# Sharing weight tiles between two streams in the input projection of a hybrid diffusion layer

## The chip, the cores and the metric

The kernel runs on one core of a Trainium2 chip. A core has five engines with instruction queues of their own, each of which is worked off in order: TensorE (PE, matmuls into the accumulator memory PSUM, with its weight loads PEld beside it), VectorE (DVE), ScalarE (ACT, activation functions with loadable tables), GpSimd (POOL, which doesn't reach PSUM) and SyncE (SP), which here issues nearly all DMAs. PSUM has eight banks of 128 x 512 float32. The metric is the time of one execution on the device in microseconds, the median of the runs.

## The reference

One layer runs on two groups of tokens with the same weights: a prompt of 256 tokens and a sample of 1024. Each has a modulation vector, a projection into 24 tiles of 128 channels and 16 dt channels, a gated short convolution, a bidirectional state space scan and an output projection, then a gated feed-forward part with a convolution. Cut to what matters here:

```python
mod_ctx = (jax.nn.silu(c_ctx)[None] @ w_ada[i] + b_ada[i])   # prompt
mod_lat = (jax.nn.silu(c) @ w_ada[i] + b_ada[i])             # sample; six blocks of 1024 each
h = rmsnorm(x, g_norm1) * (1.0 + scale_m) + shift_m
proj = h @ w_in
hc, gb, gc, z, xbc, dtf, dtb = jnp.split(proj, offs, axis=-1)
out_a = gb * dwconv1d(gc * hc, w_conv_short)
xbc = jax.nn.silu(dwconv1d(xbc, w_conv_ssd, b_conv_ssd))
xs, bm, cm = jnp.split(xbc, [SSD_WIDTH, SSD_WIDTH + SSD_GROUPS * D_STATE], axis=-1)
dt_f = jax.nn.softplus(dtf + dt_bias[0]); dt_b = jax.nn.softplus(dtb + dt_bias[1])
y_f, s_f = ssd_scan(xh, dt_f, a[0], bm, cm, init_f)
y_b_rev, s_b = ssd_scan(xh[:, ::-1], dt_b[:, ::-1], a[1], bm[:, ::-1], cm[:, ::-1], init_b)
y = rmsnorm((y_f + y_b_rev[:, ::-1] + xh * d_skip) * jax.nn.silu(z), g_ssd_norm)
x = x + gate_m * (jnp.concatenate([out_a, y], axis=-1) @ w_out)
h2 = rmsnorm(x, g_norm2) * (1.0 + scale_f) + shift_f
u = conv(h2 @ w_up); ug, uv = jnp.split(u, 2, axis=-1)
x = x + gate_f * ((jax.nn.silu(ug) * uv) @ w_down)
```

The kernel returns the normalised outputs of both streams and the prompt's two final states.

## The kernel before

Channels lie on the 128 partitions, tokens along the free dimension. Every float32 operand of a projection is split into a high part that the matmul takes in full and a low remainder, and `mm3` adds three products (high x high, high x low, low x high) over eight slices of 128 input channels. A weight tile (512 KB) is brought in by `wload`: a DMA into a "raw" tile (two buffers), a copy on ACT to the high part and a subtraction on DVE or POOL for the low part. The parts rotate over three pairs of buffers, whi and wlo twice and whx and wlx once. A prompt tile is 24 matmuls of 256 tokens, a sample tile 48 of 512.

The program is traced in the order in which it is written; a planner of the kernel language then sets the order of each engine's instructions from its own estimate of when each is ready, with the written order as priority. `after(a, b)` asks for a behind b without a wait on the chip. A tile that reuses a buffer waits until its last user is done; a pool opened on the bytes of closed pools waits for all their users, or, with `reuse_waits="tile"`, tile by tile (in PSUM: bank by bank).

The stages in question, in the order written:

- The loop over eight channel slices normalises, modulates with blocks 0 and 1 (`ada_block`), and already accumulates the sample's X tiles 0 and 1 and its dt projection. The normalised prompt lies in "bc" tiles (its high and low parts), the sample in "h".
- `xbc(SS, i)` evacuates the sample's X tiles 0 and 1: a convolution of three taps, one ACT pass and two DVE passes. PSUM then holds "acc" (two buffers of two banks), "sa" (three of one bank) and "yp" (one).
- The prompt (`SP`) runs through all its 24 tiles in a row, each with its own `wload`, staged in one of eight "x" tiles of the pool `nrm`: X, B and C (8), z (4, `zproj`), the short convolution (`outa`, 3 tiles each for j = 0 to 3). Its accumulators are "sa" for the first two and "acc" for the rest. `dtstage` computes softplus and the cumulative sums of dt (a chain of some 20 small DVE and ACT instructions on 40 partitions), `dttok` transposes them to token order on TensorE and forms the decays. For the prompt dtstage is written behind the first z tile, dttok behind `outa` 0. The sample's dtstage is written at the end.
- The sample (`SS`) runs through tiles 2 to 6 of X, B and C, with modulation blocks 2 to 5 between them (`ada`: 8 DMAs of 512 KB a block into the "x" tiles, matmuls in four column groups, and for each half of a block an ACT copy, four transposes and a reduction). dttok of the sample comes behind tile 4.
- `nrm` closes, the scan begins: `ssd_pass1(SP)`, the sample's tile 7, `ssd_pass1(SS)` and `ssd_pass2`, filled up with the sample's z and short convolution tiles (`fillers`).
- The pool ps1 closes; ps2 opens for the output projection (`wout`) and the feed-forward part.

Of the kernel before, what the change touches and what calls it, by code (L numbers as in the profile page):

```python
# [33 lines left out]
N_LOOP = 2  # L34
# [21 lines left out]
def body(nc, tc, A):  # L56
    cnt = [0]

    def T(pool, shape, tag, bufs, dt=F32):
        cnt[0] += 1  # L60
        return pool.tile(list(shape), dt, tag=tag, bufs=bufs, name=f"{tag}_{cnt[0]}")

    def open_pool(name, side="left", **kw):
        if "space" not in kw:
            kw["reuse_waits"] = "tile"
        g = tc.tile_pool(name=name, bufs=1, side=side, **kw)
        return g, g.__enter__()
# [27 lines left out]
    def smv(n):  # L95
        a, b = SMO[n]
        return sm[:, a:b]
# [26 lines left out]
    wx = [nrm]  # L124
    g_ps, ps = open_pool("ps1", space=PSUM)

    def pacc():
        return T(ps, [P, 1024], "acc", 2)

    def pst():  # L130
        return T(ps, [P, 512], "yp", 1)
# [1 line left out]
    def psa():  # L133
        return T(ps, [P, 512], "sa", 3)
# [11 lines left out]
    def wload(src, lo_eng, raw=None):  # L146
        if raw is None:
            raw = T(wst, [P, KT, P], "raw", 2)
        dma(raw, src)
        hi, lo = wpair()  # L150
        act(hi, raw, AF.Copy)  # L151
        tt(lo, raw, hi.bitcast(F32), ALU.subtract, lo_eng)
        return hi, lo
# [12 lines left out]
        return mms  # L166


    def ada(cc, wt):
        pt = [psa(), psa()]  # L170
        for k0 in (0, 4):
            ws = [wt() for _ in range(4)]
            for q, w in enumerate(ws):
                dma(w, A["w_ada"][(k0 + q) * P:(k0 + q + 1) * P, (cc - 2) * 1024:(cc - 1) * 1024])
            for i in range(2):
                for q in (3, 2, 1, 0):
                    nc.tensor.matmul(pt[i][32 * q:32 * q + 32, :], sc[:, k0 + q, :],
                                     ws[q][:, i * 512:(i + 1) * 512], start=k0 == 0, stop=k0 == 4,
                                     skip_group_check=True, tile_position=(0, 32 * q))
        ss = []  # L180
        for i in range(2):
            s = T(nrm, [P, 1024], "x", 8)
            act(s[:, 0:512], pt[i], AF.Copy)
            ss.append(s)
        yield
        for i, s in enumerate(ss):
            tp = psa()
            for b in range(4):
                mm = nc.tensor.transpose(tp[:, b * P:(b + 1) * P], s[:, b * P:(b + 1) * P], ident)
                if i == b == 0:  # L190
                    after(mm, mid_mm[0])
            b0 = cc * 8 + i * 4
# [48 lines left out]
    pr_p = pst()  # L241
    for i in range(2):
        nc.tensor.matmul(pr_p[:, 0:TP], ones, accp[:, i], start=i == 0, stop=i == 1)
    xs = [T(nrm, [P, TS], "x", 8) for _ in range(KT)]
    pr_s = [psa(), psa()]
    for k in range(KT):
        dma(xs[k], xT[:, k, TP:TT])
# [108 lines left out]

    last_mm, mid_mm = [], [None]

    def proj(s, m, lo_eng):
        g = proj_halves(s, m, lo_eng)  # L360
        next(g)
        return next(g)

    def proj_halves(s, m, lo_eng):
        s.n += 1
        wh, wl = wload(A["w_in"][m], lo_eng, T(nrm, [P, KT, P], "x", 8) if s.name == "p" else None)
        pp = psa() if s.name == "p" and s.n <= 2 else pacc()
        outs = []
        for a, b in s.chunks:
            outs.append((pp[:, a:b], (lambda k, a=a, b=b: s.hi(k)[:, a:b]),  # L370
                         (lambda k, a=a, b=b: s.lo(k)[:, a:b])))
        ks = list(range(KT))
        for half in (ks[0:KT // 2], ks[KT // 2:]):
            ends = mm3(outs, wh, wl, KT, half)
            mid_mm[0] = ends[0]
            last_mm.append(ends[-1])
            yield pp[:, 0:s.T]

    def conv1d_sb(out, u, w, n):
        stt(out[:, 1:n], u[:, 0:n - 1], w[0], out[:, 1:n], ALU.mult, ALU.add)  # L380
        stt(out[:, 0:n - 1], u[:, 1:n], w[2], out[:, 0:n - 1], ALU.mult, ALU.add)

    def xbc(s, i, out, lo_eng):
        w = [smv("wcx")[:, i * 3 + t:i * 3 + t + 1] for t in range(3)]
        b = smv("bcx")[:, i:i + 1]
        if s.name == "s" and i < N_LOOP:
            u = pps[i]
            for c in range(2):
                act(out[:, c * 512:(c + 1) * 512], u[c], AF.Identity, scale=w[1], bias=b)
            stt(out[:, 1:513], u[0], w[0], out[:, 1:513], ALU.mult, ALU.add)  # L390
            stt(out[:, 513:TS], u[1][:, 0:511], w[0], out[:, 513:TS], ALU.mult, ALU.add)
            stt(out[:, 0:511], u[0][:, 1:512], w[2], out[:, 0:511], ALU.mult, ALU.add)
            stt(out[:, 511:TS - 1], u[1], w[2], out[:, 511:TS - 1], ALU.mult, ALU.add)
        else:
            pp = proj(s, 16 + i, lo_eng)
            act(out, pp, AF.Identity, scale=w[1], bias=b)
            conv1d_sb(out, pp, w, s.T)

    def zproj(s, j, lo_eng):
        for _ in zproj_halves(s, j, lo_eng):  # L400
            pass
# [186 lines left out]
    def ssd_pass2(s, fill, post):  # L588
# [110 lines left out]
    d4_s = dtcopy(SS, pd_s)  # L699
    for i in range(N_LOOP):  # L700
        xbc(SS, i, SS.X[i], PG)
        act(SS.X[i], SS.X[i], AF.Silu)
    for i in range(8):
        xbc(SP, i, (SP.X + bcp)[i], PG if i % 3 else PV)
        if i == 5:
            pd_p = [psa()]
            dtmm(pd_p, range(KT), lambda k: xp[k // 4][:, k % 4], TP)
            d4_p = dtcopy(SP, pd_p)
    act(xall, xall, AF.Silu)
    silu = act(bcall, bcall, AF.Silu)  # L710
    for j in range(4):
        zproj(SP, j, PG if j % 2 else PV)
        if j == 0:
            dts = dtstage(SP, d4_p, silu)
    for j in range(4):
        for _ in outa(SP, j, PG):
            pass
        if j == 0:
            dttok(SP, *dts)
    dts = dtstage(SS, d4_s, silu)  # L720


    bcs = [T(sd, [P, TS], "bc", 4) for _ in range(4)]
    SS.B, SS.C = bcs[0:2], bcs[2:4]
    xbcs = SS.X + bcs

    def silu_s(i):
        after(act(xbcs[i], xbcs[i], AF.Silu), SS.last_exp)

    pend = None  # L730
    for i in range(N_LOOP, 7):
        xbc(SS, i, xbcs[i], PV)
        if pend is not None:
            next(pend)
            pend = None
        if i == 4:
            dttok(SS, *dts)
            for k in range(N_LOOP, 4):
                silu_s(k)
        if i >= 4:  # L740
            silu_s(i)
        if i < 6:
            pend = ada(i, lambda: T(nrm, [P, 1024], "x", 8))
            next(pend)
    make_aff(1, 4, "g2")
    wx[0] = None
    close_pool(g_nrm)
# [498 lines left out]
```

## Time and profile before

| | us |
|---|---|
| median of 3 runs | 1577.9 (1575.82 to 1578.37) |
| profiled execution | 1575.34 |
| its span, first to last instruction | 1573.4 |
| PE busy | 1522.2 |
| DVE busy | 1104.6 |
| ACT busy | 662.1 |
| POOL busy | 514.6 |

The profiled execution is one of the same program; its span is what the views of the trace count from. "Busy" is the time in which an engine has an instruction under way; matmuls overlap, so a matmul's own duration is longer than its share, and the distance from one start to the next tells what it costs. A row of a group or a timeline reads: line, engine, operation, out<-in by the names of tiles, shape, count, and in square brackets the idle time before it and what ended that. The granted clock is TensorE's, 1.00 at full speed.

### The profile page before, as it was taken

Reading aid. Unit: us, or ns where it says so; the run is one execution under the profiler, and the core shown is the slowest. Engines: PE = TensorE matmul, PEld = TensorE weight load, DVE = VectorE, ACT = ScalarE, POOL = GpSimd, SP = SyncE. Lnnn points to the kernel's source line nnn. Section 1 sums busy time; section 2 is a strip of 40 time slices with the busy share of each in tenths; the row PEclk is TensorE's granted clock in tenths of the full one; section 3 lists DMA queues with packets and bytes.
Section 4 is the critical chain, followed back from the end, with each engine's and each line's share of the span. In section 5 each row is a group of like instructions: output and inputs, shape, how many; then the busy total and the mean of one; then the engine's idle time right before and its main releaser. Section 6 shows DMA issues by size and latency. Waiting matters only on the chain. (4 is left out here: it accounts for less than half of the span.)

```text
span 1573.4 us, 22518 instructions
## 1 busy us (share of the span) xinstructions
PE 1522.2 (97%) x8722; PEld 1296.7 (82%) x8722; DVE 1104.6 (70%) x1634; ACT 662.1 (42%) x1025; POOL 514.6 (33%) x288
## 2 busy tenths in 40 slices
PE   6989999999999999999999999999999999999997
PEld 3688667778787888888888888898888888888886
DVE  5765615367887349796666598656679878798696
ACT  6553334257777135433322253322334433433333
POOL 1445001111120001344333333333346545455452
PEclk9999999999999999999999999999999999999999
DMA  8555554343434712222222242222252333343221
GB/s 305 215 185 167 211 203 147 110 151 132 139 116 142 287 54 102 93 74 68 69 77 74 66 143 96 73 66 67 88 173 96 97 108 95 101 161 98 94 77 61
DMA packets 86908, 191.98 MB, mean 122 GB/s; under 512 B 9330, under 2 KB 36626, under 8 KB 86802
## 3 DMA queue, kind: packets, MB, share of 16 engines
q1 hardware_dynamic: 80978, 187.41, 35.1%
q10 hardware_dynamic: 5824, 3.15, 0.7%
q8 instruction: 68, 1.11, 0.3%
q14 instruction: 38, 0.31, 0.1%
HBM read 167.37 MB, written 23.15 MB: 121 GB/s over the span
## 5 line engine op out<-in xcount | busy, mean ns | idle before, releaser
L80 DVE SCALAR_TENSOR_TENSOR cc<-acc,sm,cc 128x504 f32<-128x504 f32 (+5 forms) x836 | 545.9, 665 | 110.2 <-ACT cc L986 51.9
L77 POOL TENSOR_TENSOR wlo<-raw,whi 128x1024 fp32r<-128x1024 f32 (+2 forms) x83 | 194.0, 2337 | 666.7 <-ACT whi L151 541.6
L151 ACT ACTIVATE whi<-raw 128x1024 fp32r<-128x1024 f32 x90 | 95.1, 1057 | 240.9 <-PE acc L162 218.0
L80 DVE SCALAR_TENSOR_TENSOR x<-dn,mod,x 128x288 f32<-128x288 f32 (+2 forms) x176 | 96.1, 547 | 95.1 <-PE dn L164 94.4
L77 POOL TENSOR_TENSOR dlo<-draw,dhi 128x512 fp32r<-128x512 f32 (+1 forms) x88 | 109.0, 1239 | 90.2 <-ACT dhi L1039 88.2
L160 PE MATMUL acc<-ya,whi 128*128 128x512 f32 (+1 forms) x400 | 119.4, 356 | 3.4 <-DVE cv L77 3.4
L164 PE MATMUL acc<-ya,wlo 128*128 128x512 f32 (+1 forms) x400 | 119.5, 356 | 0.0
L162 PE MATMUL acc<-ya,whi 128*128 128x512 f32 (+1 forms) x400 | 119.5, 356 | 0.0
L164 PE MATMUL acc<-oa,wlo 128*128 128x512 f32 (+1 forms) x400 | 118.9, 355 | 0.0
L162 PE MATMUL acc<-oa,whi 128*128 128x512 f32 (+1 forms) x400 | 118.7, 354 | 0.0
L160 PE MATMUL acc<-oa,whi 128*128 128x512 f32 (+1 forms) x400 | 118.2, 353 | 0.0
L160 PE MATMUL dn<-yb,dhi 128*128 128x288 f32 (+2 forms) x352 | 110.0, 313 | 5.3 <-DVE x L80 4.1
L77 POOL TENSOR_TENSOR wlx<-raw,whx 128x1024 fp32r<-128x1024 f32 (+2 forms) x32 | 74.0, 2313 | 119.2 <-ACT whx L151 104.5
L162 PE MATMUL dn<-yb,dhi 128*128 128x288 f32 (+2 forms) x352 | 109.6, 311 | 0.8 <-POOL yb L77 0.8
L164 PE MATMUL dn<-yb,dlo 128*128 128x288 f32 (+2 forms) x352 | 109.5, 311 | 0.0
L160 PE MATMUL acc<-h,whi 128*128 128x512 f32 x320 | 104.1, 404 | 0.0
L1039 ACT ACTIVATE dhi<-draw 128x512 fp32r<-128x512 f32 (+1 forms) x88 | 53.0, 602 | 121.4 <-PE dn L162 50.0
L162 PE MATMUL acc<-h,whi 128*128 128x512 f32 x320 | 101.0, 395 | 0.0
L164 PE MATMUL acc<-h,wlo 128*128 128x512 f32 x320 | 100.1, 394 | 0.0
L160 PE MATMUL dn<-g,dhi 128*128 128x288 f32 (+2 forms) x304 | 95.1, 313 | 0.0
L162 PE MATMUL dn<-g,dhi 128*128 128x288 f32 (+2 forms) x304 | 94.7, 312 | 0.3 <-POOL g L77 0.3
L164 PE MATMUL dn<-g,dlo 128*128 128x288 f32 (+2 forms) x304 | 94.7, 312 | 0.0
(340 smaller groups left out, 3631.8 us busy)
## 6 DMA issues: line engine op xcount, KB each, us to landing
raw<-in_w_up SPq DMA_DIRECT2D x88, 512.0 KB, 3.2
x<-in_w_ada SPq DMA_DIRECT2D x32, 512.0 KB, 5.4
draw<-in_w_down SPq DMA_DIRECT2D x64, 256.0 KB, 2.7
x<-in_w_in SPq DMA_DIRECT2D x24, 512.0 KB, 3.3
raw<-in_w_in SPq DMA_DIRECT2D x22, 512.0 KB, 4.3
xs<-in_w_ad SPq DMA_DIRECT2D x16, 512.0 KB, 8.4
csb<-csds SPq DMA_DIRECT2D x16, 512.0 KB, 3.9
raw<-in_w_out SPq DMA_DIRECT2D x16, 512.0 KB, 3.2
```

What stands on the lines that cost most here:

```text
L77: (eng or V).tensor_tensor(out=out, in0=a, in1=b, op=op)
L80: V.scalar_tensor_tensor(out=out, in0=a, scalar=s, in1=b, op0=op0, op1=op1)
L151: act(hi, raw, AF.Copy)
L160: nc.tensor.matmul(o, wh[:, k, :], rh(k), start=k == 0, stop=False)
L162: nc.tensor.matmul(o, wh[:, k, :], rl(k), start=False, stop=False)
L164: mm = nc.tensor.matmul(o, wl[:, k, :], rh(k), start=False, stop=k == n - 1)
L1039: act(wh, raw, AF.Copy)
```

## The change

The sample's tiles 2 to 7 of X, B and C and the prompt's tiles of the same channels now use one loaded and split weight tile (`xbc_both`, low part always on DVE), sample first, for tile 7 prompt first. The prompt's 18 other tiles are written between them by a generator, `prompt_tiles`: X 0 and 1 and z 0 before tile 2, z 1 to 3 before tile 3, then four short convolution tiles before each of tiles 4, 5 and 6. Their weights are staged in "raw" instead of "x". Modulation blocks 2 to 5 become eight steps of 512 columns (`ada_steps`), 8 DMAs of 256 KB each into tiles "ws", one behind the first prompt tile of a group (not of the first) and one in the middle of each shared tile. dtstage of the sample comes behind the first prompt tile, its dttok in the middle of tile 2, with dtstage of the prompt behind it, and dttok of the prompt in the middle of tile 3.

PSUM has three successive pools up to the scan's end: ps1 to the sample's tile 1, ps2 for the shared stage ("sa" three, "pj" three of one bank for the prompt, "acc" one of two banks), ps3 with the old division. PSUM pools are now opened with `reuse_waits="tile"`, the one for the output projection too. Four of the sample's input tiles, and later its B and C, lie in "bcs" tiles of the pool sd; the scan's "csb" tiles take the places of the normalised prompt ("bc").

```diff
     def open_pool(name, side="left", **kw):
-        if "space" not in kw:
+        if kw.get("space") != DRAM:
             kw["reuse_waits"] = "tile"
...
     def pacc():
-        return T(ps, [P, 1024], "acc", 2)
+        return T(ps, [P, 1024], "acc", 1 if ph_p[0] else 2)
+
+    ph_p = [False]
+
+    def pj():
+        return T(ps, [P, 512], "pj", 3)
...
-    def ada(cc, wt):
-        pt = [psa(), psa()]
...
+    def ada_steps():
+
+        for e in range(8):
+            pt = psa()
+            for k0 in (0, 4):
+                ws = [T(nrm, [P, 512], "ws", 8) for _ in range(4)]
+                for q, w in enumerate(ws):
+                    dma(w, A["w_ada"][(k0 + q) * P:(k0 + q + 1) * P, e * 512:(e + 1) * 512])
                 for q in (3, 2, 1, 0):
...
+                    mm = nc.tensor.matmul(pt[32 * q:32 * q + 32, :], sc[:, k0 + q, :], ws[q],
+                                          start=k0 == 0, stop=k0 == 4, skip_group_check=True,
+                                          tile_position=(0, 32 * q))
+                    if k0 == 0 and q == 3:
+                        after(mm, mid_mm[0])
+            s = T(nrm, [P, 512], "ss", 2)
+            act(s, pt, AF.Copy)
+            yield
             tp = psa()
...
-    xs = [T(nrm, [P, TS], "x", 8) for _ in range(KT)]
+    xs = [T(nrm, [P, TS], "x", 4) if k % 2 else T(sd, [P, TS], "bcs", 4) for k in range(KT)]
...
+    def xbc_both(i, order):
+
+        wh, wl = wload(A["w_in"][16 + i], nc.vector)
+        for s in order:
+            small = s.name == "p"
+            pp = (pj() if ph_p[0] else psa()) if small else pacc()
+            outs = [(pp[:, a:b], (lambda k, a=a, b=b: s.hi(k)[:, a:b]), (lambda k, a=a, b=b: s.lo(k)[:, a:b]))
+                    for a, b in s.chunks]
+            ks = list(range(KT))
+            for half in [ks] if small else [ks[0:KT // 2], ks[KT // 2:]]:
+                ends = mm3(outs, wh, wl, KT, half)
+                mid_mm[0] = ends[0]
+                last_mm.append(ends[-1])
+                if half[-1] < KT - 1:
+                    yield
+            conv_x(s, i, pp[:, 0:s.T], s.xbc[i])
+        yield
+
+    def conv_x(s, i, pp, out):
+        w = [smv("wcx")[:, i * 3 + t:i * 3 + t + 1] for t in range(3)]
+        act(out, pp, AF.Identity, scale=w[1], bias=smv("bcx")[:, i:i + 1])
+        conv1d_sb(out, pp, w, s.T)
...
     def proj_halves(s, m, lo_eng):
         s.n += 1
-        wh, wl = wload(A["w_in"][m], lo_eng, T(nrm, [P, KT, P], "x", 8) if s.name == "p" else None)
-        pp = psa() if s.name == "p" and s.n <= 2 else pacc()
+        wh, wl = wload(A["w_in"][m], lo_eng)
+        pp = pj() if s.name == "p" else pacc()
...
-        d4 = T(wst, [P, s.T], "raw", 2) if s.name == "s" else T(cv, [P, s.T], "cv", 4)
+        d4 = T(wst, [P, s.T], "raw", 2) if s.name == "s" else T(nrm, [P, s.T], "d4p", 1)
...
-                csb = T(sw[0], [P, 8, L], "csb", 4)
+                csb = T(sd, [P, 8, L], "bc", 4)
...
-    for i in range(8):
-        xbc(SP, i, (SP.X + bcp)[i], PG if i % 3 else PV)
...
-    pend = None
-    for i in range(N_LOOP, 7):
-        xbc(SS, i, xbcs[i], PV)
...
+    close_pool(g_ps)
+    close_pool(g_nrm)
+
+
+    g_ps, ps = open_pool("ps2", space=PSUM)
+    g_nrm, nrm = open_pool("nrm2")
+    wx[0] = nrm
+    ph_p[0] = True
+    bcs = [T(sd, [P, TS], "bcs", 4) for _ in range(4)]
...
+    pd_p = [psa()]
+    dtmm(pd_p, range(KT), lambda k: xp[k // 4][:, k % 4], TP)
+    d4_p = dtcopy(SP, pd_p)
...
+    def prompt_tiles():
+        for i in range(N_LOOP):
+            xbc(SP, i, SP.X[i], PG if i % 3 else PV)
+            yield
+        for j in range(4):
+            zproj(SP, j, PG if j % 2 else PV)
+            yield
+        for j in range(4):
+            g = outa(SP, j, PG)
+            for _ in range(3):
+                next(g)
+                next(g)
+                yield
+
+    small = prompt_tiles()
+    mods = ada_steps()
+    for i, n in zip(range(N_LOOP, 7), (3, 3, 4, 4, 4)):
+        if i == N_LOOP:
+            next(small)
+            n -= 1
+            dts = dtstage(SS, d4_s, silu)
+        for t in range(n):
+            next(small)
+            if t == 0 and i > N_LOOP:
+                next(mods)
+        both = xbc_both(i, (SS, SP))
+        next(both)
+        if i == 2:
+            dttok(SS, *dts)
             dts = dtstage(SP, d4_p, silu)
...
+        if i == 3:
             dttok(SP, *dts)
...
+        next(mods)
+        next(both)
+        if i == 3:
+            silu_s(2)
+            silu_s(3)
+            act(xall, xall, AF.Silu)
         if i >= 4:
             silu_s(i)
...
+        if i == 5:
+            act(bcall[:, 0:2], bcall[:, 0:2], AF.Silu)
+    close_pool(g_ps)
+    g_ps, ps = open_pool("ps3", space=PSUM)
+    ph_p[0] = False
     make_aff(1, 4, "g2")
...
-    xbc(SS, 7, xbcs[7], PV)
+    for _ in xbc_both(7, (SP, SS)):
+        pass
+    act(bcall[:, 2:4], bcall[:, 2:4], AF.Silu)
     silu_s(7)
```

More of the change, by code (lines that the diff above doesn't have):

```diff
@@ L166, in mm3 @@
         return mms
-    def ada(cc, wt):
-        pt = [psa(), psa()]
[L171 to L175, printed above, removed]
-                for q in (3, 2, 1, 0):
[L177 to L186, printed above, removed]
+    def ada_steps():
[5 more added lines that the diff above has]
+                    dma(w, A["w_ada"][(k0 + q) * P:(k0 + q + 1) * P, e * 512:(e + 1) * 512])
+                for q in (3, 2, 1, 0):
+                    mm = nc.tensor.matmul(pt[32 * q:32 * q + 32, :], sc[:, k0 + q, :], ws[q],
[6 more added lines that the diff above has]
+            yield
             tp = psa()
@@ L189, in ada @@
                 mm = nc.tensor.transpose(tp[:, b * P:(b + 1) * P], s[:, b * P:(b + 1) * P], ident)
-                if i == b == 0:
+                if b == 0:
                     after(mm, mid_mm[0])
-            b0 = cc * 8 + i * 4
+            b0 = 16 + e * 4
             V.tensor_reduce(out=mod[:, b0:b0 + 4, :],
@@ L394, in xbc @@
         else:
-            pp = proj(s, 16 + i, lo_eng)
-            act(out, pp, AF.Identity, scale=w[1], bias=b)
-            conv1d_sb(out, pp, w, s.T)
+            conv_x(s, i, proj(s, 16 + i, lo_eng), out)
     def zproj(s, j, lo_eng):
@@ L701, in body @@
         xbc(SS, i, SS.X[i], PG)
-        act(SS.X[i], SS.X[i], AF.Silu)
-    for i in range(8):
-        xbc(SP, i, (SP.X + bcp)[i], PG if i % 3 else PV)
[L705 to L713, printed above, removed]
+        silu = act(SS.X[i], SS.X[i], AF.Silu)
@@ new lines, in body, with silu_s @@
+    close_pool(g_ps)
[5 more added lines that the diff above has]
+    bcs = [T(sd, [P, TS], "bcs", 4) for _ in range(4)]
+    SS.B, SS.C = bcs[0:2], bcs[2:4]
+    SS.xbc, SP.xbc = SS.X + bcs, SP.X + bcp
+    pd_p = [psa()]
+    dtmm(pd_p, range(KT), lambda k: xp[k // 4][:, k % 4], TP)
+    d4_p = dtcopy(SP, pd_p)
+    def silu_s(i):
+        after(act(SS.xbc[i], SS.xbc[i], AF.Silu), SP.last_exp)
+    def prompt_tiles():
[11 more added lines that the diff above has]
+                yield
@@ L714, in body @@
+    small = prompt_tiles()
[13 more added lines that the diff above has]
+            dttok(SS, *dts)
             dts = dtstage(SP, d4_p, silu)
[L715 to L718, printed above, removed]
+        if i == 3:
@@ L719, in body @@
             dttok(SP, *dts)
[L720 to L728, printed above, removed]
-    pend = None
-    for i in range(N_LOOP, 7):
-        xbc(SS, i, xbcs[i], PV)
[L733 to L739, printed above, removed]
+        next(mods)
@@ L740, in body @@
+        next(both)
[3 more added lines that the diff above has]
+            act(xall, xall, AF.Silu)
         if i >= 4:
             silu_s(i)
-        if i < 6:
-            pend = ada(i, lambda: T(nrm, [P, 1024], "x", 8))
-            next(pend)
+        if i == 5:
[3 more added lines that the diff above has]
+    ph_p[0] = False
     make_aff(1, 4, "g2")
```

## The prediction

> **What bounds the kernel now.** I read the page first, then the waits of TensorE in the first 600 us, then busy time by stage, then the timelines of the stages that the change touches.
>
> ```profile
> span 1573.4 us, 22518 instructions
> ...
> PE 1522.2 (97%) x8722; PEld 1296.7 (82%) x8722; DVE 1104.6 (70%) x1634; ACT 662.1 (42%) x1025; POOL 514.6 (33%) x288
> ```
>
> TensorE (PE) is busy 97% of the span and no other engine is near it. The change keeps every matmul, so it can win only where TensorE is idle or runs at a lower clock. The waits (who waited for whom: us, times, longest) and four stretches (length; busy us of PE, weight load, DVE, ACT, POOL; granted clock; DMA share; GB/s) tell how much that is:
>
> ```profile
> PE sa L523 <- DVE cv L520: 3.4, 1, 3.4
> PE acc L160 <- DVE cv L77: 3.4, 1, 3.4
> PE acc L160 <- ACT xl L409: 3.3, 1, 3.3
> ...
> PE acc L160 <- ACT bcp L396: 1.0, 1, 1.0
> ```
>
> ```profile
> 70.00:118.00 48.00, 43.55 (x345) 40.50 (x343) 30.22 (x44) 30.57 (x43) 24.88 (x11) 1.00 0.56 195
> 118.00:157.00 39.00, 35.58 (x269) 34.90 (x268) 20.07 (x24) 15.26 (x24) 21.91 (x9) 0.91 0.54 166
> 157.00:237.00 80.00, 79.52 (x430) 53.88 (x429) 35.85 (x57) 30.86 (x36) 0.81 (x1) 1.00 0.58 205
> 500.00:520.00 20.00, 16.61 (x80) 13.94 (x79) 7.97 (x9) 8.76 (x11) 0.00 (x0) 0.91 0.55 190
> ```
>
> From 70 to 157 us the prompt's 24 weight tiles run one after the other; from 157 to 237 the sample's tiles 2 to 6, modulation between them; at 509 us the output projection begins. The prompt's stretch is idle for 3.4 + 3.3 + 1.0 = 7.7 us, and its clock of 0.91 costs 39 x 0.09 = 3.5 us. The sample's stretch idles 80.00 - 79.52 = 0.5 us. At 509 us it is 3.4 us idle and 20 x 0.09 = 1.8 us of clock. Together 7.7 + 3.5 + 0.5 + 3.4 + 1.8 = 16.9 us, 1.1% of the time: all that the change can gain there. One tile is this much work:
>
> ```profile
> 105.31 0.28 PE L160 MATMUL acc<-bc,whi 128*128 128x256 f32 x1
> ...
> 111.07 0.28 PE L160 MATMUL acc<-bc,whx 128*128 128x256 f32 x1
> ...
> 158.51 0.74 PE L160 MATMUL acc<-h,whx 128*128 128x512 f32 x2
> ...
> 169.72 2.78 PE L177 MATMUL sa<-x,sc 128*32 128x512 f32 x24
> ```
>
> The first two rows start two prompt tiles that lie two tiles apart: 5.76 / 2 = 2.88 us each. The others enclose one sample tile: 11.2 us.
>
> **The change part by part.** *Shared weights.* Six 512 KB loads, six copies on ACT and six subtractions (four on POOL, two on DVE) go:
>
> ```profile
> L77 POOL TENSOR_TENSOR wlo<-raw,whi 128x1024 fp32r<-128x1024 f32 (+2 forms) x83 | 194.0, 2337 | 666.7 <-ACT whi L151 541.6
> L151 ACT ACTIVATE whi<-raw 128x1024 fp32r<-128x1024 f32 x90 | 95.1, 1057 | 240.9 <-PE acc L162 218.0
> ...
> 496.02 1.22 DVE L77 TENSOR_TENSOR wlo<-raw,whi 128x1024 fp32r<-128x1024 f32 x1
> ```
>
> That is 6.3 us of ACT, 9.3 of POOL, 2.4 of DVE, all of it beside matmuls: nothing by itself. But 15 POOL subtractions now lie in about 150 us of TensorE's work (18 x 2.88 + 5 x 14.1 for the tiles, 8 x 1.9 for modulation, some 10 for dt work and transposes), where 19 lay in 87. That matters because of this:
>
> ```profile
> 137.70 2.40 POOL L77 TENSOR_TENSOR wlo<-x,whi 128x1024 fp32r<-128x1024 f32 x1 [0.48 <-ACT whi L151]
> ...
> 138.05 2.85 DVE L80 SCALAR_TENSOR_TENSOR cv<-cv,sm,cv 128x255 f32<-128x255 f32 x2 [0.94 <-ACT cv L431]
> ...
> 154.97 1.00 DVE L80 SCALAR_TENSOR_TENSOR cv<-cv,sm,cv 128x255 f32<-128x255 f32 x2 [0.58 <-ACT cv L431]
> ...
> 126.24 2.35 DVE L520 TENSOR_SCALAR cv<-cst,cep 40x40 f32<-40x40 f32 x2
> ...
> 128.74 0.37 PE L523 MATMUL sa<-cv,ones 40*128 40x80 f32 x1 [3.42 <-DVE cv L520]
> ```
>
> The same two DVE instructions take 1.00 us alone and 2.85 beside a POOL subtraction, which holds DVE up until it is done. Two instructions on 40x40 took 2.35 us, and TensorE, waiting for them, 3.42.
>
> *The wait for the prompt's z copy (3.3 us)* has the same root:
>
> ```profile
> 116.71 0.42 ACT L493 ACTIVATE cv<-cv 40x256 f32<-40x256 f32 x1 [4.44 <-DVE cv L492]
> 117.03 0.36 ACT L409 ACTIVATE xl<-acc 128x256 f32<-128x256 f32 x1
> ```
>
> ACT runs in order: the logarithm of the prompt's dt stage stood at its head for 4.44 us, and behind it the copy that frees an accumulator. The change gives prompt tiles three banks of their own ("pj") where "acc" had two buffers: one more is 2.9 us of cover, so 3.3 - 2.9 = 0.4 us stay. One of the two slow-clock spells follows this wait, so I let half of the 3.5 us go with it. Gain 2.9 + 1.7 = 4.6 us. The 1.0 us, also an accumulator that comes free late, is within the same cover: gain 1.0. The sample stretch's 0.5 us goes with modulation steps of half the size: 0.5. At worst, cover that another late copy uses up, all three stay.
>
> *The two dt stages* move. The sample's starts behind the first prompt tile and its transposes (dttok) are written into the middle of sample tile 2; the prompt's starts there and ends in the middle of tile 3. A TensorE that waits for them holds up every later matmul.
>
> ```profile
> 101.78 0.63 PE L458 MATMUL sa<-cv,cst 128*40 128x256 f32 x2
> ...
> 118.70 0.42 ACT L502 ACTIVATE cv<-cv 40x256 f32<-40x256 f32 x1 [1.30 <-DVE cv L77]
> ...
> 124.88 0.44 PE L513 MATMUL sa<-cst,cv 40*128 40x40 f32 x4
> ...
> 156.67 1.91 PE L458 MATMUL sa<-raw,cst 128*40 128x512 f32 x4
> ...
> 184.84 1.06 ACT L502 ACTIVATE cv<-cv 40x1024 f32<-40x1024 f32 x1 [6.38 <-DVE cv L77]
> ...
> 201.95 1.18 PE L513 MATMUL sa<-cst,cv 40*128 40x40 f32 x16
> ```
>
> The sample's chain took 184.84 + 1.06 - 156.67 = 29.2 us and had 45.3 until its transposes. Now two prompt tiles and half a sample tile lie between: 2 x 2.88 + 5.6 = 11.4 us in the order written, so 29.2 - 11.4 = 17.8 us is the upper end of the new wait and zero the lower. Does TensorE keep the order written? From 101.78 to 124.88 are 23.1 us; less the 3.3 of waiting, 1.7 of slow clock and the 0.6 of the dt matmuls, 17.5 us or six tiles remain: four of z and two of the first short convolution, though dttok is written behind three. So the planner places the transposes where it holds them ready, here 124.88 - 119.12 = 5.8 us after the chain's real end. It errs by what POOL adds to DVE's times; the nearest row is the 3.42 us, with the other half of the clock loss 5.2. POOL will be busy 15 x 2.34 in 150 us, 23%, against 24.88 + 21.91 in 87, 54%; I take 5.2 x 0.43 = 2.3 us for each stage. The prompt's wins 5.2 - 2.3 = 2.9, the sample's loses 2.3.
>
> *Weights with two raw buffers.* The prompt's loads lose the eight "x" tiles as staging and use the two "raw" tiles. One is held for landing, copy and subtraction.
>
> ```profile
> raw<-in_w_up SPq DMA_DIRECT2D x88, 512.0 KB, 3.2
> x<-in_w_ada SPq DMA_DIRECT2D x32, 512.0 KB, 5.4
> draw<-in_w_down SPq DMA_DIRECT2D x64, 256.0 KB, 2.7
> ...
> raw<-in_w_in SPq DMA_DIRECT2D x9, 512.0 KB, 7.1
> ```
>
> At 3.2 us to landing that is 3.2 + 1.06 + 2.34 = 6.6 us, for two buffers 3.3 a tile, over TensorE's 2.88. But a group of four prompt tiles stands behind a shared tile of 11.2 + 2.9 us and a modulation step of 1.9 (16 matmuls at 2.78 / 24, the row at 169.72); in that time two more tiles are split and two loaded. Counted from its end, the third is split at 1.06 + 2.34 = 3.4 us, the fourth at 2.88 + 3.4 = 6.3; the next shared tile, loaded from 3.4 on, is ready at 3.4 + 7.1 + 1.06 + 1.22 = 12.8, even with the 7.1 us that loads beside modulation have (last row, 157 to 237 us), and is wanted at 4 x 2.88 + 1.9 = 13.4. So I take nothing; the upper end is two buffers' pace at 7.1 us, 10.5 / 2 - 2.88 = 2.4 for each of 18 tiles, 43 us.
>
> *One sample accumulator, smaller modulation steps.* Evacuating a sample tile is one ACT and two DVE passes:
>
> ```profile
> 186.75 1.19 ACT L396 ACTIVATE xs<-acc,sm 128x1024 f32<-128x1024 f32 x1
> ...
> 188.02 1.28 DVE L80 SCALAR_TENSOR_TENSOR xs<-acc,sm,xs 128x1023 f32<-128x1023 f32 x1
> ```
>
> 1.19 + 2 x 1.28 = 3.8 us lie beside three prompt tiles (8.6 us); without that cover they would cost 3.8 for each of five tiles. The eight modulation steps are the same matmuls and evacuations, their weights 64 loads of 256 KB. By the rows 2 x 2.7 - 3.2 = 2.2 us more for a pair, on a queue that is busy 54 to 58%; two steps share some 27 us, so nothing.
>
> *Start.* The sample's dt copy holds one raw buffer until its matmuls, so prompt tiles 1 and 2 load through the other: 0 to 3.3 us (one tile's pace), I take 1.0.
>
> *PSUM by bank.* New pools in PSUM now wait bank by bank. At 509 us a whole pool waits:
>
> ```profile
> 508.32 1.22 DVE L77 TENSOR_TENSOR cv<-acc,cv 128x1024 f32<-128x1024 f32 x1
> ...
> 509.69 0.59 PE L160 MATMUL acc<-ya,whi 128*128 128x256 f32 x2 [3.39 <-DVE cv L77]
> ```
>
> The output projection's first matmul waits for the last reader of the old pool; its weights were split at 496.02 + 1.22. If its banks are not that reader's, 3.4 + 1.8 = 5.2 us go. I take all of it; at worst none.
>
> Sum: -4.6 - 1.0 - 0.5 - 2.9 + 2.3 + 1.0 - 5.2 = -10.9 us. The profiled execution took 1575.3 us (span 1573.4 and 1.9 around it), which gives 1564.4. The median of the runs, 1577.9, is 2.6 higher: on that scale **1567.0 us**, and so for all times below.
>
> **The rivals.** *Half of it* (0.18): the banks collide and the 5.2 us stay: 1572.2. For it: an accumulator takes two banks of eight. Against: only one reader is late.
> *All of it* (0.10): no dt wait, no start loss, the clock full throughout: -16.9, 1561.0. For it: POOL's thinner load. Against: 2.35 us of DVE sufficed for the 3.42.
> *Loads late* (0.08): the halved loads cost 32 x 2.2 = 70 us of queue, where 150 us at 56% leave 66; the queue fills, landing passes 7.7 us, and shared tiles wait. At two buffers' best pace, 0.42 x 18 = 7.6 us, 1574.6. Against: the 2.2 us are mostly latency, which loads in flight together share. The Trainium skill, DMA: Bandwidth & Descriptors, section "Measured (HBM→SBUF, 128 partitions, SWDGE, issued from GpSimd)", speaks for this rival: it asks for 1 MiB or more in one DMA. The trace agrees that small loads are dearer by the byte (2.7 us for 256 KB, 3.2 for 512), but shows no full queue.
> *Slower* (0.12): the sample's transposes stay where they are written. TensorE waits 17.8 us in the middle of tile 2 and runs slowly for some 1.8 us after: 19.6 instead of 2.3, 1584.3. It is slower once that loss passes 2.3 + 10.9 = 13.2 us, that is, with the transposes less than some 18 us behind the dt matmuls. For it: the distance shrinks from 45.3 us to 11.4. Against: the placing at 124.88.
>
> **How the numbers follow.** My forecast has 0.52. Faster by over 0.2% (3.2 us, about what a measurement of this kernel can tell from no change) are the forecast, half and all of it: 0.80. Late loads lie at that border and count as the same: 0.08. Slower: 0.12. The range leaves out the slower case: from 1557 (all of it, and a quarter more for waits outside the four stretches) to 1577 (the late loads, with the start at its worst).
>
> **What would show it.** Right: no wait over 1 us for xl or bcp; an output projection that starts within 1 us of the last convolution matmul; waits of 1 to 4 us at L513 or L523's successors; 70 us to the first state transposes some 6 us shorter. Wrong: matmuls of a shared or prompt tile that wait for whi, wlo or a weight DMA; over 13 us at the sample's transposes; matmuls that wait for "acc" or "pj" behind ACT.

## The result and the profile after

| | before | after |
|---|---|---|
| median (us) | 1576.6 (1573.89 to 1578.37, 6 runs) | 1584.7 (1582.31 to 1585.33, 6 runs) |
| span of the profiled execution | 1573.4 | 1583.3 |
| granted clock, whole span | 0.993 | 0.989 |

The ratio is 1.0051, 95% interval [1.0038, 1.0064]: the change makes the kernel 8.1 us slower. The prediction said 10.9 us faster, and the time lies above its range. The median of the kernel before moved between 1575.8 and 1576.6 from one series of runs to the next; sizes of effects below are therefore taken from ratios, one thousandth being 1.58 us. Each ratio is known to 1 to 2 thousandths, so a difference of two ratios is clear only from about 3 us on. The ratios leave out one slow run of an experiment, 2513.7 us at a granted clock of 0.557.

The page of the kernel after, its first lines:

```profile
span 1583.3 us, 22535 instructions
...
PE 1526.7 (96%) x8722; PEld 1301.9 (82%) x8722; DVE 1095.8 (69%) x1632; ACT 656.7 (41%) x1020; POOL 504.0 (32%) x284
```

The matmuls are the same 8722, and each of the other engines lost work, as the diff said. Waits of TensorE in the kernel after, from 60 to 560 us (in total, times, longest):

```profile
PE pj L165 <- ACT whx L156: 5.1, 1, 5.1
PE sa L538 <- DVE cv L77: 3.0, 1, 3.0
PE acc L165 <- DMA oa<-oad: 2.9, 1, 2.9
...
PE pj L165 <- ACT whi L156: 1.7, 1, 1.7
PE sa L183 <- DMA ws<-in_w_ada: 1.7, 1, 1.7
PE sa L563 <- ACT btok L565: 1.7, 1, 1.7
PE acc L165 <- ACT whx L156: 1.4, 1, 1.4
PE pj L169 <- POOL wlo L77: 0.5, 1, 0.5
PE pj L169 <- DVE wlx L77: 0.5, 1, 0.5
```

All four waits that the prediction counted in the kernel before (xl, bcp, the decays at L523, the projection's on DVE) are gone from the list. New ones stand in their place: first weight tiles, the sample's dt transposes, weights of modulation, and a load of oa (a short convolution tile, read back from its copy oad in DRAM). Two stretches of both kernels (length; busy us of PE, weight load, DVE, ACT, POOL; granted clock; DMA share; GB/s), first before, then after:

```profile
72.00:135.00 63.00, 55.13 (x421) 52.14 (x420) 37.17 (x52) 35.68 (x52) 30.17 (x14) 0.95 0.55 186
135.00:245.00 110.00, 109.44 (x648) 81.95 (x647) 55.27 (x76) 43.45 (x56) 16.99 (x7) 1.00 0.59 204
```

```profile
72.00:135.00 63.00, 49.16 (x293) 38.54 (x288) 41.83 (x66) 32.52 (x45) 9.24 (x4) 0.89 0.52 172
135.00:245.00 110.00, 108.33 (x719) 89.14 (x718) 41.35 (x57) 39.78 (x55) 29.05 (x13) 1.00 0.56 194
```

Idle time and lost clock from 72 to 245 us were 7.9 + 63 x 0.05 + 0.6 = 11.6 us before. After they are 13.8 + 63 x 0.11 + 1.7 = 22.4: 10.8 us more, nearly all of it in the first 63 us. From 135 us on the new order runs as smoothly as the old one (one wait, for btok). Matched by their place counted from the program's end, the matmuls run 0.2 us behind those of before at 69 us, 10.5 at 245 and 10.0 at the end; in between the distance falls to 5.2 at 523 us, where the projection no longer waits, and is 10.9 again at 542.

**The start of the shared stage.** Three timelines of the kernel after. First SyncE's DMA queue:

```profile
44.94 6.51 SPq L284 DMA_DIRECT2D xs<-in_w_ad  x4
72.23 0.33 SPq L181 DMA_DIRECT2D ws<-in_w_ada  x1
72.66 0.37 SPq L154 DMA_DIRECT2D raw<-in_w_in  x1
73.09 3.33 SPq L181 DMA_DIRECT2D ws<-in_w_ada  x7
79.39 16.10 SPq L154 DMA_DIRECT2D raw<-in_w_in  x5
```

From 51.5 to 72.2 us the queue issues nothing. At its head stands a modulation load ("ws"), whose bytes belong to the sample's x tiles until their last dt matmul; behind it waits the first prompt tile's weight load. Then ScalarE:

```profile
69.48 1.45 ACT L416 ACTIVATE xs<-acc,sm 128x512 f32<-128x512 f32 x2 [3.88 <-PE acc L336]
72.37 1.08 ACT L475 ACTIVATE raw<-sa 128x512 f32<-128x512 f32 x2 [1.44 <-PE sa L307]
73.34 1.45 ACT L416 ACTIVATE xs<-acc,sm 128x512 f32<-128x512 f32 x2
74.81 1.28 ACT L727 ACT_TABLE_LOAD   x1
76.11 1.06 ACT L727 ACTIVATE xs<-xs 128x1024 f32<-128x1024 f32 x1
77.07 1.04 ACT L156 ACTIVATE whx<-raw 128x1024 fp32r<-128x1024 f32 x1
```

The copy that makes the first tile's high part comes at 77.07, behind the evacuations, a table load and a Silu; it goes to whx. And TensorE:

```profile
72.04 1.05 PE L307 MATMUL sa<-xl,toks 128*32 128x256 f32 x12
78.16 0.58 PE L165 MATMUL pj<-bc,whx 128*128 128x256 f32 x1 [5.07 <-ACT whx L156]
...
79.80 0.42 PE L165 MATMUL pj<-bc,whx 128*128 128x256 f32 x1
...
87.56 0.28 PE L165 MATMUL pj<-bc,whi 128*128 128x256 f32 x1
...
111.10 0.28 PE L538 MATMUL sa<-cst,cv 40*128 40x40 f32 x2 [2.96 <-DVE cv L77]
```

After 5.07 us of waiting the same matmul takes 0.42 us where it later takes 0.28: the clock has dropped (granted clock 0.50 from 78.2 to 84.4 us). The second prompt tile's load goes out at 79.39, since the sample's dt copy holds the other raw buffer ("raw<-sa" above). Five waits for weights add up to 5.1 + 0.5 + 0.5 + 1.7 + 1.4 = 9.2 us.

**The output projection.** TensorE and the DMA queue in the kernel after:

```profile
516.54 0.51 PE L165 MATMUL acc<-ya,whi 128*128 128x256 f32 x2
...
529.30 1.01 PE L165 MATMUL acc<-oa,whi 128*128 128x256 f32 x2 [2.88 <-DMA oa<-oad]
...
534.58 0.78 PE L165 MATMUL acc<-oa,whi 128*128 128x256 f32 x2
535.20 0.52 PE L167 MATMUL acc<-oa,whi 128*128 128x256 f32 x2
```

```profile
521.07 0.32 SPq L468 DMA_DIRECT2D oad<-xl  x1
523.38 0.32 SPq L469 DMA_DIRECT2D oad<-xl  x1
...
524.26 2.39 SPq L920 DMA_DIRECT2D oa<-oad  x2
```

The projection starts at 516.54 without a gap. But the last short convolution tile still has to go out to DRAM (521.07, 523.38) and come back (from 524.26), and TensorE runs out of other products. It waits 2.88 us, until 529.30, and then goes at half speed until 535.2 (granted clock 0.50 from 529.3).

### The profile page after: what moved, and what is told of

The parts are those of the page before. It is cut to its first block, busy times and chain, and to the rows that moved or that the text cites. A ratio compares the mean times of both kernels' runs of the same rounds, so it can differ in the third digit from the quotient of the medians.

```text
span 1583.3 us, 22535 instructions
## 1 busy us (share of the span) xinstructions
PE 1526.7 (96%) x8722; PEld 1301.9 (82%) x8722; DVE 1095.8 (69%) x1632; ACT 656.7 (41%) x1020; POOL 504.0 (32%) x284
## 5 line engine op out<-in xcount | busy, mean ns | idle before, releaser
L77 POOL TENSOR_TENSOR wlo<-raw,whi 128x1024 fp32r<-128x1024 f32 (+2 forms) x93 | 217.7, 2342 | 674.3 <-ACT whi L156 594.9
L156 ACT ACTIVATE whi<-raw 128x1024 fp32r<-128x1024 f32 x102 | 107.8, 1057 | 250.7 <-PE acc L167 212.1
L77 POOL TENSOR_TENSOR wlx<-raw,whx 128x1024 fp32r<-128x1024 f32 (+2 forms) x37 | 86.0, 2325 | 168.5 <-ACT whx L156 153.8
L165 PE MATMUL acc<-ya,whi 128*128 128x512 f32 (+1 forms) x400 | 119.5, 356 | 0.0
```

What stands on the lines that cost most here:

```text
L77: (eng or V).tensor_tensor(out=out, in0=a, in1=b, op=op)
L165: nc.tensor.matmul(o, wh[:, k, :], rh(k), start=k == 0, stop=False)
```

## The experiments

**Each half of the projection's story by itself.** Theory: the gain of the bank-wise PSUM wait was given back to that round trip. Rival: bank-wise waits are worth their 5 us, and something else ate them. First the kernel after with the old, pool-wide wait there:

```diff
-            kw["reuse_waits"] = "tile"
+            kw.setdefault("reuse_waits", "tile")
...
-    g_ps, ps = open_pool("ps2", space=PSUM)
+    g_ps, ps = open_pool("ps2", space=PSUM, reuse_waits="pool")
```

> The changed kernel, but the output projection's PSUM pool waits for the whole old pool again, as before the change. Theory 'round trip': the 3.4 us wait in front of the projection comes back, the 2.9 us wait for oa<-oad goes, and the time is the same within 2 us. Rival 'bank by bank saves it': 5 us slower than the changed kernel.

Measured: 1585.5 us, ratio 1.0062 [1.0049, 1.0075]. Then the kernel before with the bank-wise wait at that one place:

```diff
-    g_ps, ps = open_pool("ps2", space=PSUM)
+    g_ps, ps = open_pool("ps2", space=PSUM, reuse_waits="tile")
```

> The kernel before with that one edit of the change: the output projection's PSUM pool waits bank by bank. Theory 'round trip': the 3.4 us wait turns into a wait of about 3 us for oa<-oad some 13 us later, and the time is that of the kernel before within 2 us. Rival 'bank by bank saves it': 5 us faster than the kernel before.

Measured: 1574.4 us, ratio 0.9989 [0.9978, 1.0000]. The edit is worth 1.1 thousandths, 1.7 us, in either kernel, which is at the edge of the noise; 5 us it is in neither. The only wait of TensorE from 490 to 560 us in each run shows the exchange; first the kernel after with the pool-wide wait, then the kernel before with the bank-wise one:

```profile
PE acc L165 <- DVE cv L77: 3.4, 1, 3.4
```

```profile
PE acc L160 <- DMA oa<-oad: 2.9, 1, 2.9
```

3.4 us on DVE are traded for 2.9 on the round trip. So the round trip can be taken out of the way instead: the kernel after, where the first three output tiles take slices 0 to 6 first and slice 7, which comes from the last short convolution tile, behind all three.

```diff
-            mm3(outs, wh, wl, KT)
+            if t0 == 0 and m < 3:
+                mm3(outs, wh, wl, KT, range(KT - 1))
+                held.append((m, pp, outs, wh, wl))
+                if m < 2:
+                    continue
+            else:
+                mm3(outs, wh, wl, KT)
+                held.append((m, pp, None, None, None))
+            for m, pp, outs, wh, wl in held:
+                if outs is not None:
+                    mm3(outs, wh, wl, KT, [KT - 1])
...
```

> The changed kernel with nothing else but the output projection's first three tiles taking slice 7 last. Theory: the 2.9 us wait for the load of oa is gone and the slow clock behind it, so that what the bank-wise PSUM wait was forecast to give is seen: 3 to 6 us less than 1584.7, 1579 to 1582. Rival (the clock takes it): 1583 to 1586.

Measured: 1581.0 us, ratio 1.0030 [1.0020, 1.0039], 3.3 us less than the kernel after by the ratios. The wait for oa is gone, and a wait of 1.0 us for a low part (wlo, by DVE) is new. Theory held, near the lower end of its 3 to 6 us.

**The order of the loads.** Theory: the modulation load at the head of SyncE's queue starves the start. The first step's loads are asked to stand behind the second prompt weight load.

```diff
-        dma(raw, src)
+        raw_dma.append(dma(raw, src))
...
-                    dma(w, A["w_ada"][...])
+                    d = dma(w, A["w_ada"][...])
+                    if e == 0:
+                        after(d, raw_dma[1])
```

> The changed kernel, but the first modulation load (ws, which waits for the old input tiles until about 72 us) is put behind the first two weight loads of the prompt in SyncE's queue. Theory 'head of the queue': the first weight load is issued near 57 us instead of 72.7, the first prompt matmul starts near 72 instead of 78.2, and 5 to 9 us of the changed kernel's 8 us loss go (about 1577 us). Rival 'one raw buffer' (the sample's dt copy holds the other one): only the first tile comes earlier, the waits move to tiles 2 and 3, and less than 3 us go. Rival 'dt transposes' (they wait 3.0 us at 111 us and set the end of the stage): no change within 2 us.

Measured: 1581.6 us, ratio 1.0037 [1.0026, 1.0049], 2.2 us less than the kernel after where the theory had 5 to 9, and not clear of noise. The first weight load went out at 57.8 us, 15 earlier, yet the first prompt matmul still waited 5.1 us for ACT's whx, which again came behind the Silu at 77.2. The queue's head was one lock of several on the same door.

**The raw buffer.** The sample's dt copy gets a tile of another tag, so that both raw buffers are free.

```diff
-        d4 = T(wst, [P, s.T], "raw", 2) if s.name == "s" else ...
+        d4 = T(sd, [P, s.T], "bcs", 4) if s.name == "s" else ...
```

> The changed kernel, but the sample's dt copy lies in a bcs tile, so that both raw buffers serve the prompt's weights from the start; the planner then puts three weight loads ahead of the first modulation load by itself. If queue and raw buffer both count: no wait over 1 us for whi, whx, wlo or wlx in the prompt's first tiles and 9 to 13 us less than the changed kernel (1572 to 1576 us). If the head of the queue is all of it: the same as with the load put behind, within 2 us. If the dt transposes set it: no change within 2 us.

Measured: 1579.3 us, ratio 1.0023 [1.0011, 1.0036], 4.4 us less than the kernel after, less than half of the 9 to 13 expected if queue and raw buffer both count, and 2.2 less than with the loads alone moved, which is not clear of noise. With two buffers free the planner put three weight loads ahead of the modulation loads by itself (54.6, 57.9 and 72.4 us). But the first tile still waited, 2.6 us for whx and 2.4 for wlx.

**The pair of buffers.** Why whx? The pairs rotate, and the prompt's first tile is the ninth weight tile: it falls on the third pair, which lies in the pool opened behind the loop, on bytes that the x tiles hold until 72 us. The second pair, whi and wlo, was free some 6 us earlier (in the run above a copy to whi starts at 66.36, the one to whx at 74.92). So the rotation is shifted by one from there on: first with the order of the loads alone, then with the dt copy elsewhere too.

```diff
-        if wx[0] is not None and wn[0] % 3 == 0:
+        if wx[0] is not None and wn[0] % 3 == (2 if ph_p[0] else 0):
```

> The changed kernel with the first modulation step's loads behind the second prompt weight load, and the rotation of weight pairs shifted by one once the prompt's tiles begin, so that the first prompt tile takes the pair whi/wlo, which is free, and not whx/wlx, which lies in the new pool on bytes that the sample's x tiles hold until their dt matmuls end at 72 us. The sample's dt copy still holds a raw buffer. Theory (the pair's bytes hold up the first tile, the one raw buffer the second): the 5.1 us wait for whx is gone and the first prompt matmul starts by 72 us, but the second tile's still waits for its load, whose buffer comes free when the dt copy has been read; 1 to 6 us below the run with the loads alone moved (1581.6): 1576 to 1580. Rival (ACT's queue is what is late, with the sample's evacuations and the table load ahead of the copy): first matmul still at 77 to 79 us, 1581 to 1583.

Measured: 1586.4 us, ratio 1.0054 [1.0036, 1.0071]: no better than the kernel after. This was a miss of the theory. ScalarE's timeline of this run shows why:

```profile
77.45 1.28 ACT L730 ACT_TABLE_LOAD   x1
78.74 1.06 ACT L730 ACTIVATE xs<-xs 128x1024 f32<-128x1024 f32 x1
79.71 1.04 ACT L157 ACTIVATE whi<-raw 128x1024 fp32r<-128x1024 f32 x1
```

The load had been issued at 60.2 us and the pair was another, but the planner had put the copy behind the table load and the Silu as before. This run's stage lies some 2.5 us later on the time axis than the others', but the distance is the same: the copy starts 7.6 us after the sample's first evacuation (72.12), as in the run with the loads alone moved (69.66 to 77.25) and in the kernel after (69.48 to 77.07), and the wait is 5.1 us in all three. Where ACT's order is kept, a free buffer gives nothing. That is the rival's mechanism; its time, 1581 to 1583, was too low as well. Why the planner kept it there with one raw buffer and not with two isn't shown. With both:

> The same with the sample's dt copy in a tile of its own, so that both raw buffers are free: loads ahead, free pair, two raw buffers. Theory: of the waits of 5.1, 0.5, 0.5, 1.7 and 1.4 us at the start of the shared stage none is left over 1 us and no slow-clock rows follow them; 1571 to 1575, the time of the kernel before less its two removed waits and plus the projection's round trip. Rival (what the start gives is lost again at the next wait, the dt transposes, which then waits longer): the wait at the sample's dt transposes grows from 2.6 us to over 6 us, 1577 to 1580.

Measured: 1575.2 us, ratio 0.9994 [0.9982, 1.0007]: the same as before the change, and 9.0 us less than the kernel after. The run with the dt copy alone moved has its first three weight loads ahead of modulation as well; against it, it is the rotation that gives 4.6. All five waits for weights are gone; but the wait at the sample's transposes has grown from 3.0 to 8.2 us. So the theory's time was met, at its upper edge, and the rival's mechanism is there too:

```profile
PE sa L541 <- DVE cv L77: 8.2, 1, 8.2
PE acc L166 <- DMA oa<-oad: 2.8, 1, 2.8
```

**Start and projection together.** The reordered projection on top of it:

> The same with the output projection's first three tiles taking their products with slices 0 to 6 first, and slice 7, whose short convolution comes back through DRAM last, behind all three. Theory (the gain of the bank-wise PSUM wait was given back to that round trip): the 2.9 us wait for the load of oa is gone, and the slow clock behind it; 4 to 6 us below the kernel with the free start alone: 1566 to 1570. Rival (the clock takes the gain: the projection runs at the same mean speed whatever waits stand in it): no more than 2 us below it.

Measured: 1571.0 us, ratio 0.9963 [0.9950, 0.9976], 4.9 us less than without it, as the theory had it. TensorE's timeline of this run against the one of the kernel after above:

```profile
72.03 1.05 PE L310 MATMUL sa<-xl,toks 128*32 128x256 f32 x12
73.02 0.38 PE L166 MATMUL pj<-bc,whi 128*128 128x256 f32 x1
...
76.07 1.91 PE L486 MATMUL sa<-bcs,cst 128*40 128x512 f32 x4
...
104.32 0.43 PE L541 MATMUL sa<-cst,cv 40*128 40x40 f32 x2 [8.32 <-DVE cv L77]
```

The last group of the dt projection starts at the same 72.0 us in both. The first prompt matmul comes 5.1 us earlier, the transposes 111.10 - 104.32 = 6.8. What now sets their time is the dt chain, 104.32 - 76.07 = 28.2 us, and DVE's timeline of the same run shows it busy with the chain, among other small work, from 84.46 us on:

```profile
84.46 1.22 DVE L80 SCALAR_TENSOR_TENSOR cv<-cv 40x1024 f32<-40x1024 f32 x1
...
97.77 2.28 DVE L512 TENSOR_TENSOR_SCAN cv<-cv,cv 40x1024 f32<-40x1024 f32 x1
...
100.66 2.28 DVE L513 TENSOR_TENSOR_SCAN cv<-cv,cv 8x1024 f32<-8x1024 f32 x1
...
103.06 1.21 DVE L77 TENSOR_TENSOR cv<-cv,cv 40x1024 f32<-40x1024 f32 x1
```

Ahead of that the chain does have slack, as ScalarE's timeline of the run shows:

```profile
78.91 1.04 ACT L730 ACTIVATE xs<-xs 128x1024 f32<-128x1024 f32 x1
...
81.76 1.06 ACT L157 ACTIVATE whi<-raw 128x1024 fp32r<-128x1024 f32 x1 [1.54 <-DMA raw<-in_w_in]
...
83.18 1.25 ACT L489 ACTIVATE cv<-sa,rows 40x512 f32<-40x512 f32 x2
```

The dt matmuls end at 76.07 + 1.91 = 77.98, but ACT takes up their result (L489) only at 83.18, 5.2 us later, behind a Silu and a weight copy that itself waited 1.54 us for its load. In the kernel after, where these matmuls come at 84.42, ACT follows them at once, and the chain takes 26.7 us. What another order on ACT would give was not tried.

**The dt transposes.** Both sets are written half a shared tile later:

```diff
-        if i == 2:
-            dttok(SS, *dts)
-            dts = dtstage(SP, d4_p, silu)
-        if i == 3:
-            dttok(SP, *dts)
         next(mods)
         next(both)
+        if i == 2:
+            dttok(SS, *dts)
+            dts = dtstage(SP, d4_p, silu)
+        if i == 3:
+            dttok(SP, *dts)
```

> The same with both sets of dt transposes (sample's and prompt's) half a shared tile later, behind the sample's second half, 5.6 us. Theory: the wait of 2.6 to 3.0 us at the sample's transposes is gone, and none over 1 us comes at the prompt's: 2 to 4 us below the kernel without it, 1563 to 1567. Rival (the prompt's dt stage then ends later than its transposes, since it starts behind the sample's): a wait of 2 to 6 us at the prompt's transposes takes its place, and the time is the same within 2 us.

Measured: 1571.3 us, ratio 0.9963 [0.9949, 0.9978]: no change. The written half tile moved them by only 17 prompt matmuls, 2 us: in the kernel with the free start the planner had already put them behind the whole sample tile. TensorE still waited 4.2 and 2.2 us, both at the sample's transposes, and not at the prompt's as the rival had it. So they go a whole group later, the sample's behind two more prompt tiles and a modulation step, the prompt's and the Silus behind it likewise:

```diff
             if t == 0 and i > N_LOOP:
                 next(mods)
+            if t == 1 and i == 3:
+                dttok(SS, *dts)
+                dts = dtstage(SP, d4_p, silu)
+            if t == 1 and i == 4:
+                dttok(SP, *dts)
...
-        if i == 2:
-            dttok(SS, *dts)
-            dts = dtstage(SP, d4_p, silu)
-        if i == 3:
-            dttok(SP, *dts)
...
-        if i == 3:
+        if i == 4:
             silu_s(2)
             silu_s(3)
             act(xall, xall, AF.Silu)
```

> The kernel with the free start and the reordered projection (1571.0 us), and both sets of dt transposes a group later: the sample's behind two more prompt tiles and a modulation step after the shared tile where they stood, the prompt's likewise one group on, with the Silus that follow it. Theory (the sample's dt chain is DVE's, 27 us from its matmul to the transposes' last operand, and its transposes stand 8.3 us too early once the start is free): that wait is gone, the wait of 2.6 us for the weights of modulation behind it too, and no new one over 1 us: 7 to 11 us less, 1560 to 1564. Rival (the prompt's chain and the Silus behind it move too, and are late for the scan's first pass): waits of 3 us and more where the scan begins, 1568 to 1572.

Measured: 1565.2 us, ratio 0.9933 [0.9921, 0.9945], the fastest kernel of the study, 0.7% under the one before. Its only long wait of the stage, and the stretch from 72 us:

```profile
PE sa L186 <- DMA ws<-in_w_ada: 3.4, 1, 3.4
```

```profile
72.00:135.00 63.00, 59.55 (x382) 45.99 (x373) 41.84 (x66) 33.56 (x47) 12.53 (x5) 0.97 0.64 208
```

It took 4.7 us off where 7 to 11 were expected: the 8.3 us are gone, but the modulation step now comes earlier against its loads and waits 3.4. The rival's waits of 3 us and more where the scan begins did not come. The same edit on the kernel after, alone:

> The changed kernel with nothing else but both sets of dt transposes a group later. Theory: its wait of 3.0 us at the sample's transposes and the 1.7 us for the weights of modulation behind it go, with the slow clock after them; the start stays: 3 to 7 us less than the changed kernel's 1584.7, 1578 to 1582. Rival (the wait is only moved on): 1583 to 1586.

Measured: 1577.9 us, ratio 1.0013 [1.0002, 1.0025], 6.0 us less than the kernel after. No wait is left at the transposes, and 0.5 us at the modulation weights. Theory held.

Side by side: the free start -9.0, the transposes -6.0, the projection -3.3, each by itself on the kernel after, add up to -18.3 us; all three together gave -18.6 (1.0051 to 0.9933). With some 3 us of uncertainty in each, the three accounts don't overlap much.

## Why the prediction was wrong

*z copy, bcp, the two raw buffers' pace.* Right as mechanisms, though what each gave was not measured by itself. No matmul waits for xl or bcp; from the second group on no tile waits over 1 us for whi, wlo or a weight load. The rival that loads come late did not happen there; only a modulation step waited 1.7 us.

*"The sample's dt copy holds one raw buffer until its matmuls, so prompt tiles 1 and 2 load through the other: 0 to 3.3 us (one tile's pace), I take 1.0."* This is the step that failed most. It saw the one buffer and priced it in tiles' pace, as if everything else were ready. Three things were not looked at: the queue that the weight loads stand in (the modulation loads, moved ahead, wait at its head for the x tiles), the pair of buffers that the ninth weight tile falls on, and ACT's order, where the copy stood behind evacuations, table load and Silu. All wait for the same moment, the last dt matmul at 72 us, so that DMA or evacuations, copy and subtraction follow one another with TensorE idle: 9.2 us of waits and a slow clock after them. Matmuls that wait for whi are what the prediction itself named as a sign of being wrong. Freeing the start was worth 9.0 us even though the transposes then waited 5.2 longer; the whole loss ahead of them is larger. The prediction looked at the moved modulation loads for the bandwidth that they take, not for their place in the queue.

*Dt stages: sample +2.3, prompt's 2.3 left.* The kind was right, a few us of waiting at transposes that the planner places close to the chain's end: 3.0 us measured where 2.3 was taken, and the rival of 17.8 was far off. The prompt's wait vanished. But the sum was mis-sized twice over. The wait is short only because the start was late; with a free start it is 8.2. And the edit that removes it is worth 6.0 us, for the clock is low after it (0.81 from 111 to 120 us, 1.7 us of the 9) and the modulation loads are 1.7 us late behind it. The cause named for it, POOL holding up DVE, is not what sets it: the sample's chain took 29.2 us before, with POOL busy 0.81 us in the whole stretch from 157 to 237 (a row of the prediction), and in the run with the free start and the reordered projection 28.2, with POOL busy 7.2 of the 40 us from 72 to 112.

*PSUM by bank: "If its banks are not that reader's, 3.4 + 1.8 = 5.2 us go. I take all of it; at worst none."* Mechanism right, gain wrong: the projection starts at once, but its next operand is late. Asking "what is late next" there would have met the store and load of the last short convolution tile in the DMA queue. Measured: 1.7 us in place of 5.2. With the projection reordered as well, which the change does not do, it is 1.7 + 3.3 = 5.0.

*The slower case.* It had 0.12, and its time, 1584.3, is almost the one measured, by a mechanism that did not occur. The sign was missed because the start's worst case was bounded by one tile's pace. It is luck likewise that the repaired kernel, 10.6 us below the one before, comes near the 10.9 forecast: it adds an edit of the projection and a later place for the transposes, which the forecast did not have.

*What stays open.* The three sizes differ from the forecast's by 9.0 - 1.0, 6.0 - 2.3 and 5.2 - 1.7, together 15.2 of the 10.9 + 8.1 = 19.0 us between forecast and result. The other 3.8 us are hardly more than the uncertainty, and no run takes them apart.

## What to carry to other kernels

When work moves to a stage's start, write down for its first tile every resource in turn (queue position, staging buffer, destination buffer, place in each engine's order), and when each is released; the last one sets the start, and freeing another one shows little. A removed wait gains only up to the next operand's arrival, so look for that operand before taking the gain. And place a serial chain's consumer by the time the chain takes (27 to 29 us here, its waits in the engines' queues included), not by the work that happens to lie between.

## What the runs showed of the hardware

In the kernel after, a wait of 2.88 us was followed by 5.9 us of matmuls at a granted clock of 0.50 (529.30 to 535.20), so that it cost about twice its length. The Trainium skill, TensorE: Matmul & The Clock Gate, section "HAM oscillation — how this bites in real kernels", warns of gaps over about 3.4 us. Here one shorter than that was enough. So was one of 2.64 us in the run with the dt copy alone moved: it ended at 106.85, and from 109 to 119 us the granted clock was 0.50 to 0.52. But one of 2.55 us, at 119.5 us in the run with the free start and the reordered projection, left the clock at 1.00:

```profile
112.00:135.00 23.00, 20.45 (x147) 14.74 (x143) 7.98 (x25) 8.67 (x17) 0.58 (x1) 1.00 0.75 247
```

What decides between them the runs don't show.
